# GLA values and GLA gate columns by one 2x2 Strassen product, with the tokens stationary

## The chip, the cores and the metric

The kernel runs on one NeuronCore of a Trainium2 chip. The metric is the device time of one execution in microseconds (us); a few executions are made and their median is given.

## The reference, cut to what matters

One encoder layer on 512 tokens of width 1024. The normalized tokens u meet one wide weight matrix w_in, whose columns feed three branches: gated linear attention (GLA), forgetting attention (FoX), and cross attention into 256 memory tokens. The branches are merged by gates, projected, and a squared-ReLU MLP follows. All of it is float32. For this change, these lines matter:

```python
u = rmsnorm(h, g_mix[l])
proj = u @ w_in[l]
(gq, gk, gv, gg, ga, fq, fk, fv, ff, mq, gates) = split_cols(proj, PROJ_SIZES)
...
o_gla = rmsnorm(o_gla, g_gla_head[l]) * jax.nn.silu(gg.reshape(B, S, GLA_HEADS, GLA_DV))
y_gla = o_gla.reshape(B, S, GLA_V) @ w_gla_o[l]
```

gv (the GLA values) and gg (the GLA output gate) are 512 columns each, for 4 heads of 128. The values enter the attention of each head; its output is normalized per token and head, scaled by a learned gain per channel, and multiplied by silu(gg).

## The kernel before

**Precision by three products.** Every float32 operand of a large product is split into a high part, rounded to the multiplication type float32r, and a low part, the rest. `mm3` (line 163) multiplies high by high, high by low and low by high into one PSUM bank. Of a weight chunk (128 partitions x 1024 numbers, 512 KB), `split_w` (line 150) makes the high part on ScalarE (line 154) and the low part on VectorE (line 155). `load_w` (line 144) loads it through SyncE's (SP's) DMA queue. The pool `weights` has three buffers each for raw, high and low chunks. The tokens u lie in SBUF as high and low halves, `uhi` and `ulo`, transposed: 8 tiles of 128 channels by 512 tokens.

**Two forms of projection.** `gT` (line 168) keeps the weights stationary and streams the 512 tokens: a chunk holds 128 output columns for all 1024 channels, 8 steps of three matmuls. `gN` (line 178) keeps the tokens stationary and streams 512 weight columns: a chunk holds 256 channels of 512 columns, and four chunks make the product for four token tiles. Both are generators that give way after three matmuls; such a step is called a unit.

**The order of the work.** TensorE's instructions run in the order in which the program writes them. `weave` (line 201) does that: it takes a list of steps of an attention branch, and between them draws units from a chain of projections, so many as the steps' shares say. The other engines, the DMA queues of SP and GpSimd (POOL) among them, are put in order by a scheduler at build time, except in stretches marked `in_order`. An instruction may be placed early there, as far as its buffers are free.

The weave of each of the three stages is one call. Lines 754, 865 and 1008:

```python
weave([partial(fn, i) for fn, i, _ in steps], 80, fox_pair(2), gla_k(0), fox_pair(3), gla_q(0), gvg,
...
weave([partial(fn, i) for fn, i, _ in steps], 48, gla_g(0, mp, "th"), gla_g(1, mp, "th"),
      outputs("w_fox_o", ofh, ofl, acc), shares=[n for *_, n in steps])
...
weave([partial(fn, *a) for fn, a, _ in steps], 64, gla_k(1), gla_q(1),
      outputs("w_mem_o", omh, oml, ymem), gla_g(2, lp, "og"), gla_g(3, lp, "og"), shares=[n for *_, n in steps])
```

- FoX (72 to 167 us): 80 units, the last 32 of them the GLA values (`gvg`, line 746, copied out of PSUM by ScalarE).
- Memory attention (167 to 233 us): 48 units, 16 of them the gate columns of two heads.
- GLA (233 to 299 us): 64 units, 16 of them the gate columns of the other two heads.

`gla_g` (line 787) is the gate: a `gT` product of 128 columns, tanh on ScalarE (line 790), and two passes of VectorE (791, 792) that make silu times gain in `sg`, channels on the partitions. In the GLA stage `gla_values` (line 955) makes the heads' outputs with tokens on the partitions and scales each row (line 977) with a reciprocal root from POOL (line 974); `gla_turn` (line 979) transposes them, multiplies by `sg` (line 985) and splits the product for the output projection. `states` (line 921) and `gla_values` read the values `gv`.

**Sums in DRAM.** The branch gates and the MLP are Strassen products already. Their weight sums for the MLP are made in DRAM by transfers in POOL's queue: `sum_ops` (line 107) lists 40, plain copies (line 126) and accumulating ones (line 124) of 0.5 or 1 MB. `next_sum` (line 116) issues them at the pace of the weight splits: none up to the 7th, two with each up to the 16th, one with each from there on. 35 are issued before the branch gates' last round. `u_sum` (line 798) makes the token sums for the branch gates in the memory stage, and `u_lefts` (line 998) and `sum_three` (line 1192) make others from them.

After the GLA stage come the rounds of the branch gates, whose first two weight chunks (`gate_ready`, line 990) are split at the end of the GLA stage.

## Time and profile before

| | |
|---|---|
| three runs | 803.93, 805.38, 807.12 us; median 805.38 |
| the profiled execution | 806.5 us, of which its span from first to last instruction is 804.7 |
| granted TensorE clock | 0.998 of full speed |
| instructions | 11704 |
| chain that ended last | TensorE 89%, VectorE 4%, DMA 3% |
| DMA queues, share of the 16 engines | POOL's (q0) 36.2%, SP's (q1) 33.9%, ScalarE's (q10) 1.4% |

In rows of the profile an engine (PE is TensorE, PEld its weight load, DVE VectorE, ACT ScalarE, POOL GpSimd, SP SyncE) stands with the line of the kernel that recorded the instruction, then output<-input by the program's names, the shape, and a count. Times are us from the start of the span, and us of duration. "idle before" is time in which the engine did nothing before that instruction, and what ended it. A line in a helper, such as 154 or 164, serves many callers.

### The profile page before, as it was taken

What the parts mean: (1) busy time and instruction counts of PE and PEld (TensorE: products, weight loads), DVE (VectorE), ACT (ScalarE), POOL (GpSimd) and SP (SyncE); (2) the same over time, 40 slices, a digit from 0 to 9 for tenths busy, and PEclk for the clock granted to TensorE, in tenths of its full rate; (3) what the DMA queues carried; (4) which work ended last, traced back from release to release, by engine and by line L of the source; (5) the groups of instructions that cost most, each with busy time, mean ns of one, the idle gap of its engine ahead of it and who ended that gap; (6) DMA issues with size and microseconds to landing.
All of it is one profiled execution on the core that took longest, in us unless ns stands there. A gap on an engine that the chain in (4) does not pass through costs nothing.

```text
span 804.7 us, 11704 instructions
## 1 busy us (share of the span) xinstructions
PE 794.1 (99%) x4375; PEld 680.0 (85%) x4375; DVE 601.5 (75%) x951; ACT 459.6 (57%) x733; POOL 91.5 (11%) x129
## 2 busy tenths in 40 slices
PE   9999999999999999999999999999999999999996
PEld 7778888888888878788888889977998899889985
DVE  6877888465654788667764758788799788988896
ACT  7857566443553355556531546864666476647764
POOL 0000102100110122121110000011001100100011
PEclk9999999999999999999999999999999999999999
DMA  9344889994594569797979514998767956795653
GB/s 356 142 157 166 330 299 240 250 287 182 128 235 161 224 194 210 235 219 204 204 163 315 171 58 169 277 237 207 236 182 186 239 206 172 192 283 190 157 89 121
DMA packets 41065, 166.49 MB, mean 207 GB/s; under 512 B 4912, under 2 KB 5616, under 8 KB 38640
## 3 DMA queue, kind: packets, MB, share of 16 engines
q0 software_dynamic: 11072, 62.92, 36.2%
q1 hardware_dynamic: 28576, 98.86, 33.9%
q10 hardware_dynamic: 1360, 3.96, 1.4%
q8 instruction: 34, 0.56, 0.3%
q14 instruction: 23, 0.19, 0.1%
HBM read 163.59 MB, written 35.68 MB: 248 GB/s over the span
## 4 chain that ended last, share of the span: by engine, by line
PE 89%; DVE 4%; DMA 3%; issue 2%; ACT 1%; POOL 1%; POOLq 0%; DVEq 0%; ACTq 0%
PE mm L164 16%; PE mm L165 15%; PE mm L166 15%; PE mm L1330 15%; PE a L165 5%; PE a L166 5%; PE a L164 5%; PE mm L1659 3%; PE mm L385 1%; DMA b<-in_wst_dram 1%; PE mm L1660 1%; PE a L398 1%; PE a L661 1%; DMA raw<-in_wst_dram 1%; PE a L700 1%
## 5 line engine op out<-in xcount | busy, mean ns | idle before, releaser
L155 DVE TENSOR_TENSOR wlo<-raw,whi 128x1024 fp32r<-128x1024 f32 x38 | 46.5, 1223 | 39.4 <-ACT whi L154 39.3
L1389 ACT CAST hi<-raw 128x1024 fp32r<-128x1024 f32 x52 | 54.5, 1048 | 37.5 <-PE mm L1330 17.7
L1390 DVE TENSOR_TENSOR lo<-raw,hi 128x1024 fp32r<-128x1024 f32 x52 | 63.5, 1221 | 14.2 <-ACT hi L1389 13.9
L1330 PE MATMUL mm<-u,hi 128*128 128x256 f32 x384 | 65.1, 283 | 0.0
L154 ACT CAST whi<-raw 128x1024 fp32r<-128x1024 f32 x38 | 39.9, 1050 | 41.2 <-PE mm L165 15.9
L164 PE MATMUL mm<-uhl,whi 128*128 128x512 f32 x144 | 57.7, 400 | 0.0
L1330 PEld LDWEIGHTS mm<-u,hi 128*128 128x128 f32 x384 | 56.8, 191 | 0.3
L166 PE MATMUL mm<-uhl,wlo 128*128 128x512 f32 x144 | 56.3, 391 | 0.0
L165 PE MATMUL mm<-uhl,whi 128*128 128x512 f32 x144 | 56.1, 390 | 0.0
L1709 POOL DMA_DIRECT2D b<-in_wst_dram x30 | 25.7, 856 | 263.4 <-DVE lo L1390 132.9
L165 PE MATMUL mm<-lo,ch 128*128 128x512 f32 (+1 forms) x132 | 51.2, 388 | 0.4 <-DVE lo L1390 0.4
L164 PE MATMUL mm<-hi,ch 128*128 128x512 f32 (+1 forms) x132 | 50.9, 386 | 0.0
L166 PE MATMUL mm<-hi,cl 128*128 128x512 f32 (+1 forms) x132 | 50.9, 386 | 0.0
L1330 PE MATMUL mm<-u2s,hi 128*128 128x256 f32 x288 | 47.6, 283 | 0.0
L1330 PE MATMUL mm<-u,lo 128*128 128x256 f32 x192 | 47.5, 283 | 0.0
L1389 ACT CAST hi<-b 128x1024 fp32r<-128x1024 f32 x26 | 27.2, 1048 | 29.3 <-PE mm L166 18.9
L1330 PEld LDWEIGHTS mm<-u2s,hi 128*128 128x128 f32 x288 | 41.8, 192 | 0.3
L1390 DVE TENSOR_TENSOR lo<-b,hi 128x1024 fp32r<-128x1024 f32 x26 | 31.7, 1221 | 10.7 <-ACT hi L1389 10.7
L165 PE MATMUL a<-lo,ch 128*128 128x512 f32 (+1 forms) x96 | 37.1, 386 | 0.4 <-DVE lo L1447 0.4
L1095 DVE TENSOR_TENSOR lo<-wb,hi 128x1024 fp32r<-128x1024 f32 x21 | 25.3, 1222 | 15.6 <-ACT hi L1091 15.6
L164 PE MATMUL a<-hi,ch 128*128 128x512 f32 (+1 forms) x96 | 37.0, 385 | 0.0
L166 PE MATMUL a<-hi,cl 128*128 128x512 f32 (+1 forms) x96 | 36.9, 385 | 0.0
(506 smaller groups left out, 2296.3 us busy)
## 6 DMA issues: line engine op xcount, KB each, us to landing
raw<-in_wst_dram SPq DMA_DIRECT2D x110, 512.0 KB
raw<-T SPq DMA_DIRECT2D x32, 512.0 KB
b<-in_wst_dram POOLq DMA_DIRECT2D x32, 512.0 KB, 5.4
T<-in_wst_dram POOLq DMA_DIRECT2D x12, 1024.0 KB, 12.6
wb<-in_wst_dram POOLq DMA_DIRECT2D x24, 512.0 KB, 7.8
b<-in_wst_dram SPq DMA_DIRECT2D x16, 512.0 KB
T<-in_wst_dram POOLq DMA_DIRECT2D x12, 512.0 KB, 8.5
wb<-in_wst_dram SPq DMA_DIRECT2D x12, 512.0 KB
```

The lines of the kernel that those rows point to most:

```text
L154: cast = nc.scalar.copy(hi, raw)
L155: low_now[0] = nc.vector.tensor_tensor(lo, raw, f(hi), op=ALU.subtract).ins
L164: nc.tensor.matmul(ps, lh, rh, start=start, stop=False, skip_group_check=on)
L165: nc.tensor.matmul(ps, lh, rl, start=False, stop=False, skip_group_check=on)
L166: nc.tensor.matmul(ps, ll, rh, start=False, stop=stop, skip_group_check=on)
L385: nc.tensor.matmul(kps[h], w[:, h * P:(h + 1) * P], x[:, k, :], start=k == p == 0, stop=k == KT - 1 and p == 2)
L1095: nc.vector.tensor_tensor(lo, source(r, c), f(hi), op=ALU.subtract)
L1330: nc.tensor.matmul(ps[:, a, :], x[:, a, k, :], y[:, s, k, :], start=start, stop=stop, skip_group_check=go is not None)
L1389: split_now[0] = nc.scalar.copy(hi, raw).ins
L1390: split_now[1] = nc.vector.tensor_tensor(lo, raw, f(hi), op=ALU.subtract).ins
L1659: nc.tensor.matmul(ps, wh[:, a, k, :], u[:, k], start=k == 0, stop=False, skip_group_check=True)
L1709: nc.gpsimd.dma_start(to[i], wst[index["B", q, i, x]], accum_op=ALU.add)
```

## The change

The two blocks of 512 columns, gate (gg) and values (gv), are taken as the two column halves of one matrix, the channels as its two row halves, and the tokens as two halves of 256. The 2x2 product is then made from seven products of half size instead of eight (Strassen's scheme in its form with few additions). Each of the seven, `linear(n, left)`, keeps token tiles stationary and streams 512 weight columns: two chunks of weights, two token tiles, 24 matmuls.

- Three products use chunks of w_in as they are (1, 2 and 3), four use weight sums G1 to G4 (2 x 512 KB each) that eight new transfers in POOL's queue make in DRAM. `first_ops` places them among the first of the MLP's sums.
- On the tokens' side, products 1, 2 and 4 use u's halves as they are; 5, 6, 7 and 3 use sums of them, which are added on VectorE and split again. `u_sum`, unchanged in what it computes, is called in the FoX stage now, so its pool opens before FoX. The sums for 7 and 3 are made in the memory stage, in buffers of that stage.
- Products 1, 5, 2, 6 replace the values in FoX's weave (32 units, as before). Products 7 and 3 replace two gate heads in the memory stage's weave (16 units, as before). Product 4 replaces two gate heads in the GLA stage's weave, which goes from 64 to 56 units.
- Evacuation: 1, 2 and 5 are copied by ScalarE; 6, 7, 4 and 3 are added or subtracted by VectorE. Product 2 goes on in product 1's PSUM banks.
- The gate has its tokens on the partitions now. silu is made there by tanh (ScalarE) and one pass of VectorE for each token tile (`gate_half`). It is multiplied in with the row scaling of `gla_values`; the gain, per channel, comes after the transposition in `gla_turn`, where ScalarE makes the high part and one pass of VectorE the low part.
- The gate columns of w_in are stored as four "N" chunks instead of four "T" chunks.

The diff, cut to its core:

```diff
+    def linear_ops():
+        for n, src, add in ((1, "11", 0), (3, "12", 0), (1, "12", 1), (3, "22", 1), (2, 1, 0), (2, "22", 1), (4, 2, 0), (4, "21", 1)):
...
+            yield gsum[n], src, add
...
+    def first_ops():
+        ff, lin = islice(sum_ops(), 35), linear_ops()
+        for own, others in ((2, 0), (1, 1), (1, 1), (1, 2), (1, 2), (1, 2), (1, 26)):
+            yield from islice(lin, own)
+            yield from islice(ff, others)
+        yield from ff
...
+    def factor_tiles():
+        return [gp.tile([P, 4, 256], F32R, tag=tag, name=nm("s")) for tag in ("gv0", "sg2")]
...
+    def linear(n, left):
+        def weights(c):
+            raw = wp.tile([P, 1024], F32, tag="raw", name=nm("raw"))
+            if n in (1, 2, 3):
+                rows, col = {1: (0, "gg"), 2: (4, "gg"), 3: (4, "gv")}[n]
+                src = wst[index["N", "w_in", rows + 2 * c, OFF[col]]]
+            else:
+                src = gsum[{5: 1, 6: 2, 7: 3, 4: 4}[n]][c]
+            nc.sync.dma_start(raw, src)
+            return [x.rearrange("p (k c) -> p k c", k=2) for x in split_w(raw)]
...
+            u, low, high = first_part[t], gv[t], gv[2 + t]
+            if n == 1:
+                nc.scalar.copy(u, ps)
+            if n == 2:
+                nc.scalar.copy(sg[t], ps)
+            if n == 5:
+                nc.scalar.copy(high, ps)
+            if n == 6:
+                vec(u, u, ps)
+            if n == 7:
+                vec(sg[2 + t], u, ps)
+                vec(low, high, u, ALU.subtract)
+                vec(high, high, sg[2 + t], ALU.subtract)
+            if n == 4:
+                vec(sg[2 + t], sg[2 + t], ps)
+            if n == 3:
+                vec(low, low, ps)
...
+        pss = kept[n] = kept[1] if n == 2 else [mmt() for _ in range(2)]
+        for c in range(2):
+            wh, wl = weights(c)
+            for t in range(2):
+                sl = slice(t * P, t * P + P)
+                for kk in range(2):
+                    k = 2 * c + kk
+                    mm3(pss[t], left[0][:, k, sl], left[1][:, k, sl], wh[:, kk, :], wl[:, kk, :], k == 0 and n != 2, k == 3, n in (1, 2))
...
+    def gate_half(t, tt):
+        nc.scalar.activation(tt, sg[t], AF.Tanh, scale=0.5)
+        nc.vector.scalar_tensor_tensor(sg[t], tt, 1.0, sg[t], op0=ALU.add, op1=ALU.mult)
...
-        weave([partial(fn, i) for fn, i, _ in steps], 80, fox_pair(2), gla_k(0), fox_pair(3), gla_q(0), gvg,
+        weave([partial(fn, i) for fn, i, _ in steps], 80, fox_pair(2), once(u_sum, 1), gla_k(0), fox_pair(3), once(early_split, 1),
+              gla_q(0), linear(1, A11r), once(u_sum, 2), linear(5, lambda: early[1]), linear(2, A12r), once(early_split, 2), linear(6, lambda: early[2]),
...
+        temps = {3: other_sum(3)}
+        other(3)
+        def linears():
+            yield from linear(7, s34[3])
+            fo = outputs("w_fox_o", ofh, ofl, acc)
+            temps[4] = other_sum(4)
+            other(4)
+            yield from islice(fo, 16)
+            yield from linear(3, s34[4])
+            gate_halves((0, 1), mp, "th")
+            yield from fo
-        weave([partial(fn, i) for fn, i, _ in steps], 48, gla_g(0, mp, "th"), gla_g(1, mp, "th"),
-              outputs("w_fox_o", ofh, ofl, acc), shares=[n for *_, n in steps])
+        weave([partial(fn, i) for fn, i, _ in steps], 48, linears(), shares=[n for *_, n in steps])
...
-                    nc.vector.tensor_scalar(on[:, t, :], po[e][:, t, :], r[:, t:t + 1], None, op0=ALU.mult)
+                    nc.vector.scalar_tensor_tensor(on[:, t, :], po[e][:, t, :], r[:, t:t + 1], sg[t][:, h * P:(h + 1) * P],
+                                                   op0=ALU.mult, op1=ALU.mult)
...
-            og = lp.tile([P, S], F32, tag="og", name=nm("og"))
-            nc.vector.tensor_tensor(og, pt, sg[h], op=ALU.mult)
-            split(ogh[h], ogl[h], og)
+            nc.scalar.mul(ogh[h], pt, gain_half[:, h:h + 1])
+            nc.vector.scalar_tensor_tensor(ogl[h], pt, gain_half[:, h:h + 1], f(ogh[h]), op0=ALU.mult, op1=ALU.subtract)
...
-        weave([partial(fn, *a) for fn, a, _ in steps], 64, gla_k(1), gla_q(1),
-              outputs("w_mem_o", omh, oml, ymem), gla_g(2, lp, "og"), gla_g(3, lp, "og"), shares=[n for *_, n in steps])
+        weave([partial(fn, *a) for fn, a, _ in steps], 56, gla_k(1), gla_q(1), linear(4, A22r), once(gate_halves, (2, 3), lp, "og"),
+              outputs("w_mem_o", omh, oml, ymem), shares=[n for *_, n in steps])
```

`once` calls a function when the weave reaches it and draws no unit.

More of the change, by code (lines that the diff above doesn't have):

```diff
@@ L45, in chunk_list @@
     L += [("N", "w_in", 2 * j, OFF["gv"]) for j in range(4)]
-    for n, c in (("gg", 4), ("mq", 4)):
-        L += [("T", "w_in", OFF[n] + P * j) for j in range(c)]
+    L += [("N", "w_in", 2 * j, OFF["gg"]) for j in range(4)]
+    L += [("T", "w_in", OFF["mq"] + P * j) for j in range(4)]
     for g, o in (("gate_fox", "w_fox_o"), ("gate_mem", "w_mem_o"), ("gate_gla", "w_gla_o")):
@@ L250, in hybrid_block, with pair_of @@
     gqT = [gp.tile([P, S], F32, name=f"gqT{j}") for j in range(2)]
-    gv = gp.tile([P, NT, 512], F32, name="gv")
-    sg = [gp.tile([P, S], F32, name=f"sg{j}") for j in range(4)]
+    gv, sg = [None] * NT, [None] * NT
+    def pair_of(rows, name, t):
+        x = gp.tile([P, 2, 512], F32, tag=f"{name}{t}", name=nm(name))
+        rows[t:t + 2] = [x[:, i] for i in range(2)]
+    def factor_tiles():
+        return [gp.tile([P, 4, 256], F32R, tag=tag, name=nm("s")) for tag in ("gv0", "sg2")]
+    for t in (0, 2):
+        pair_of(gv, "gv", t)
+        pair_of(sg, "sg", t)
     ofh = [ofp.tile([P, S], F32R, name=f"ofh{j}") for j in range(4)]
@@ L414, in hybrid_block @@
             mem_keys(k)
-        macc, rm = gv[:, 2, :M], gv[:, 1, :2]
-        msq = [gv[:, j, :] for j in range(4)]
+        macc, rm = gv[2][:, :M], gv[1][:, :2]
+        msq = gv[:]
         ms, rx = (small(fp, NT, g) for g in ("ms", "rx"))
@@ L497, in mem_split @@
                                                op1=ALU.subtract)
+    mst = ExitStack()
+    edge = mst.enter_context(pool("edge", side="right"))
+    edge.tile([P, 112], F32, name="edge_pad")
+    xsp = mst.enter_context(pool("sums", side="right"))
+    xsum = {n: xsp.tile([P, 4, 256], F32, name=f"x{n}") for n in (1, 2)}
+    A11r, A12r, A21r, A22r = ([t[:, 4 * k:4 * k + 4, 256 * i:256 * i + 256] for t in (uhi, ulo)] for i in range(2) for k in range(2))
+    A11, A12, A21, A22 = ([f(t) for t in a] for a in (A11r, A12r, A21r, A22r))
@@ new lines, in u_sum, with once @@
+    def u_sum(n):
+        x = xsum[n]
+        if n == 1:
+            nc.vector.tensor_tensor(x, A21[0], A22[0], op=ALU.subtract)
+            nc.vector.tensor_tensor(x, x, A21[1], op=ALU.add)
+            nc.vector.tensor_tensor(x, x, A22[1], op=ALU.subtract)
+        else:
+            nc.vector.tensor_tensor(x, xsum[1], A11[0], op=ALU.subtract)
+            nc.vector.tensor_tensor(x, x, A11[1], op=ALU.subtract)
+    def once(fn, *args):
+        fn(*args)
+        yield from ()
+    kept = {}
@@ L764, in hybrid_block, with om_tile @@
     ogp = mst.enter_context(pool("ogla", side="right"))
-    xsp = mst.enter_context(pool("sums", side="right"))
     omst = ExitStack()
     omp = omst.enter_context(pool("omem", side="right"))
-    omt = [omp.tile([P, 2, S], F32R, tag=f"om{j}", name=f"om{j}") for j in range(4)]
-    omh, oml = ([x[:, i] for x in omt] for i in range(2))
+    omh, oml = {}, {}
+    def om_tile(j):
+        x = omp.tile([P, 2, S], F32R, tag=f"om{j}", name=f"om{j}")
+        omh[j], oml[j] = (x[:, i] for i in range(2))
     def half_of(t, c):
@@ L886, in hybrid_block @@
         stat = small(lp, LINE, "stat")
+        gain_half = stat[:, 64:68]
+        nc.scalar.mul(gain_half, ghead, 0.5)
         def decays(j):
```

74 lines of the change are left out of this document (46 added, 28 removed).

## The prediction

> **What bounds the kernel now.** I read the page first, then TensorE's waits, its pace, and the engines and DMA by stage.
>
> ```profile
> PE 794.1 (99%) x4375; PEld 680.0 (85%) x4375; DVE 601.5 (75%) x951; ACT 459.6 (57%) x733; POOL 91.5 (11%) x129
> ```
>
> Matmul ends are modelled, so 99% alone proves little. The list of what TensorE waited for is complete in four lines:
>
> ```profile
> PE a L296 <- DVE warm L293: 1.2, 1, 1.2
> PE mm L164 <- ACT hi L1091: 0.7, 1, 0.7
> PE a L165 <- DVE lo L1447: 0.4, 1, 0.4
> PE mm L165 <- DVE lo L1390: 0.4, 1, 0.4
> ```
>
> That is 2.7 us in 804.7, none of it in the lines that the change touches. TensorE's own work sets the time, and a removed matmul is worth its pace, not its 390 ns duration. The pace, from two rows of one unbroken stretch:
>
> ```profile
> 238.29 0.39 PE L164 MATMUL mm<-uhl,whi 128*128 128x512 f32 x1
> ...
> 242.82 0.39 PE L166 MATMUL mm<-uhl,wlo 128*128 128x512 f32 x1
> ```
>
> Twenty starts lie between them: (242.82 - 238.29) / 20 = 0.2265 us for a matmul of 512 columns. What the other engines have free, by stage (FoX is from 72 to 167, memory 167 to 233, GLA 233 to 299; the columns after the window and its length are PE, weight loads, DVE, ACT, POOL, clock, DMA share, GB/s):
>
> ```profile
> 40.00:72.00 32.00, 31.89 (x153) 25.44 (x153) 22.64 (x51) 18.91 (x35) 1.56 (x1) 1.00 0.49 166
> 72.00:118.00 46.00, 46.00 (x269) 38.48 (x266) 41.00 (x136) 30.34 (x79) 5.11 (x10) 1.00 0.78 286
> 131.00:167.00 36.00, 36.00 (x191) 30.29 (x190) 18.30 (x47) 18.05 (x37) 5.42 (x7) 1.00 1.03 246
> 167.00:233.00 66.00, 66.00 (x331) 55.95 (x330) 39.48 (x70) 30.66 (x68) 6.07 (x10) 1.00 0.67 201
> 274.00:299.00 25.00, 25.00 (x133) 20.61 (x131) 20.29 (x32) 12.64 (x18) 5.62 (x4) 1.00 0.53 147
> ```
>
> Two things stand out: all 16 DMA engines are full from 131 to 167, and VectorE is busy 20.29 of the last 25 us of GLA.
>
> **The matmuls.** Values and gate columns cost 96 matmuls each now (4 chunks x 24), 192 in all. Seven products of 24 are 168. FoX keeps its 80 woven units (32 of values become products 1, 5, 2, 6) and memory its 48 (two gate columns become 7 and 3). GLA goes from 64 to 56 (two gate columns become product 4). So 24 x 0.2265 = 5.44 us go, all in GLA. The Trainium skill, "TensorE: Matmul & The Clock Gate", section "Wait — 56ns, not 53.3ns?", gives N / 2.4 GHz + 2.5 ns, 215.7 ns at 512 columns: by it the saving would be 5.18. The rows are 5% slower, and the measurement decides. Nothing before the profiled execution's 804.7 us span or behind it changes: 1.8 us lie around it in 806.5, and the median of the runs, 805.38, is 1.1 lower.
>
> **VectorE and ScalarE.** The prices:
>
> ```profile
> L155 DVE TENSOR_TENSOR wlo<-raw,whi 128x1024 fp32r<-128x1024 f32 x38 | 46.5, 1223 | 39.4 <-ACT whi L154 39.3
> L985 DVE TENSOR_TENSOR og<-a,sg 128x512 f32<-128x512 f32 x4 | 2.8, 690 | 1.2 <-PE a L983 0.9
> L791 DVE SCALAR_TENSOR_TENSOR sg<-tt,mm 128x512 f32<-128x512 f32 x4 | 2.7, 681 | 0.7 <-ACT tt L790 0.7
> L1001 DVE TENSOR_TENSOR x<-x,uhl 128x1024 f32<-128x1024 f32 x2 | 2.4, 1218 | 0.0
> L792 DVE TENSOR_SCALAR sg<-sg,cols_s 128x512 f32<-128x512 f32 x4 | 1.9, 480 | 0.0
> L154 ACT CAST whi<-raw 128x1024 fp32r<-128x1024 f32 x38 | 39.9, 1050 | 41.2 <-PE mm L165 15.9 <-issue 12.9 <-PE mm L166 10.0
> L746 ACT COPY gv<-mm 128x512 f32<-128x512 f32 x4 | 2.4, 589 | 2.6 <-PE mm L166 2.6
> ```
>
> FoX gets on VectorE five token-sum passes, moved here from memory (5 x 1.22), two low parts of sums (2.4), four more chunk splits (4.9) and product 6's additions (2 x 0.68): 14.8 us. On ScalarE it gets six casts and two evacuations: 6 x 1.05 + 2 x 0.59 = 7.5. The sums need only the normalized tokens, and 9.4 us of VectorE lie free from 40 to 72 and 17.7 from 131 to 167, so I count nothing. The cover is gone if they fall between 72 and 118, where 5.0 are free: then up to 14.8 - 5.0 = 9.8.
>
> Memory on VectorE: minus the five passes (6.1) and two old gate evacuations (2 x (0.68 + 0.48) = 2.3); plus four passes for the other sums (4.9), two low parts (2.4), two more chunk splits (2.4), eight evacuation passes and two gate halves (10 x 0.68). That is +8.1 in 66 us with 26.5 free: nothing. Weights through ScalarE rise by two casts, again with room.
>
> GLA on VectorE: product 4's two additions and two gate halves (2.7) against two old gate evacuations (2.3) and four multiplications at L985 (2.8): lighter by 2.4. The row scaling at L977 becomes a form with one more operand; no row shows it at 128 columns. I take no difference, since that step is short; 16 instructions at even double their 0.28 would add 4.5, and they are part of the chain below.
>
> **The end of GLA.** Here the cover shrinks.
>
> ```profile
> 279.52 0.94 PE L965 MATMUL a<-mid,qpos 64*128 64x128 f32 x12
> ...
> 287.35 0.80 PE L983 MATMUL a<-cst_s,on 128*128 128x128 f32 x4
> ...
> 292.79 0.60 PE L983 MATMUL a<-cst_s,on 128*128 128x128 f32 x4
> ```
>
> ```profile
> 286.64 1.13 DVE L977 TENSOR_SCALAR on<-a,stat 128x128 f32<-128x128 f32 x4 [0.31 <-POOL stat L974]
> ...
> 289.87 1.13 DVE L977 TENSOR_SCALAR on<-a,stat 128x128 f32<-128x128 f32 x4 [0.30 <-POOL stat L974]
> ```
>
> Ten units stand between head 2's values and its transposes, which begin at 287.35 while L977 still writes their last slices (to 287.77): no slack. With shares of 61, the old order gives 64x55//61 - 64x45//61 = 57 - 47 = 10 units, the new one 50 - 41 = 9; behind it 7 become 6. Each is 3 x 0.2265 = 0.68 less cover. Between 0 (the 2.4 us that VectorE loses lie in this chain) and 1.4 I take 0.6. The second gate_fox chunk now takes the buffer of a w_mem_o chunk that is read until two units before the end; 2 x 0.68, the transposes (0.6) and the six matmuls of the first chunk (1.36) leave 3.3 us for a split of 2.3. It costs nothing, or up to 2.3 if ScalarE's queue is late.
>
> **The weights in FoX.** This is the large unknown. Values take their 96 matmuls from 136.0 to 162.7 (one of three is at L164):
>
> ```profile
> 136.00:162.70 26.70, 12.65 (x32) 5.93 (x32) 1.00 1.04 245
> ```
>
> They need 4 chunks in that time; the four products need 8, one in 3.3 us. How fast SP's queue (q1) can bring 512 KB beside POOL's sums (q0) is in this window, 142.5 to 154.5 (packets, MB, share of the engines):
>
> ```profile
> q0 software_dynamic: 290, 2.00, 80.0%
> q1 hardware_dynamic: 277, 1.04, 22.9%
> ```
>
> 1.04 MB in 12 us is two chunks, 6.0 us each, the two queues taking turns one for one (290 to 277 packets). A load is issued when the low part of three chunks earlier has freed its buffer:
>
> ```profile
> 138.06 1.22 DVE L155 TENSOR_TENSOR wlo<-raw,whi 128x1024 fp32r<-128x1024 f32 x1
> ...
> 139.31 6.44 SPq L147 DMA_DIRECT2D raw<-in_wst_dram  x2
> ```
>
> That split belongs to the third chunk behind the point where values start, so five chunks are issued before 139 in either kernel. The sixth would start at 142.5, where the old one's packets start, and land at 148.5, the next at 154.5, 160.5, 166.5, 172.5; with 1.05 + 1.22 for the split they are ready at 150.8, 156.8, 162.8, 168.8, 174.8. TensorE's order wants them at 152.3, 157.6, 160.3, 164.5 and 169.9 (the last two are memory queries of 5.4 us each). Late by 0, 0, 2.5, 4.3, 4.9: 4.9 us of stall if the sums press all the time. Do they? The change puts eight transfers of 1 MB into POOL's queue ahead of the feed-forward sums:
>
> ```profile
> 80.81 1.24 POOL L126 DMA_DIRECT2D T<-in_wst_dram  x2 [14.56 <-ACT whi L154]
> 84.48 0.97 POOL L126 DMA_DIRECT2D T<-in_wst_dram  x2 [2.43 <-ACT whi L154]
> 93.44 0.97 POOL L126 DMA_DIRECT2D T<-in_wst_dram  x2 [8.00 <-ACT whi L154]
> 103.19 0.97 POOL L126 DMA_DIRECT2D T<-in_wst_dram  x2 [8.78 <-ACT whi L154]
> 111.52 0.97 POOL L126 DMA_DIRECT2D T<-in_wst_dram  x2 [7.37 <-ACT whi L154]
> 121.39 1.65 POOL L124 DMA_DIRECT2D T<-in_wst_dram  x2 [8.90 <-ACT whi L154]
> 127.24 1.65 POOL L124 DMA_DIRECT2D T<-in_wst_dram  x2 [4.20 <-ACT whi L154]
> 138.32 1.63 POOL L124 DMA_DIRECT2D T<-in_wst_dram  x2 [9.43 <-ACT whi L154]
> ...
> 164.78 0.52 POOL L126 DMA_DIRECT2D T<-T  x1 [5.13 <-ACT whi L154]
> ```
>
> L126 is plain copies, L124 adds. Two go with each split up to the 16th, then one. The first row is the eighth split. G1 and G3 take it and a place each at 84 and 93, G2 one at 103 and one at 111, G4 one at 127 and one at 138; so the splits of 121 and 127 carry copies instead of adds, and nothing is piled up at 138. From 138 to 167 the queue holds 3 MB of copies, G4's add and 3 MB of old adds. At 2.0 MB in 9.6 us of engine time an add costs 4.8 per MB; a copy costs 2.95, worked out below; six loads cost 1.4 each: 8.9 + 19.2 + 8.2 = 36 us of work in 29. So it presses, but without a backlog at the start. Between 0 and 4.9 I take 2.4.
>
> **Sum.** -5.4 + 0.6 + 2.4 = -2.4: the profiled execution goes from 806.5 to 804.1, the median from 805.4 to **803.0**.
>
> **Rivals.** *Loads in time* (nothing late in FoX): for it speaks that no load delayed TensorE at 1.03 DMA share before, casts running about three chunks ahead. 805.4 - 5.4 + 0.6 = 800.6.
>
> *Loads late all the way* (4.9 with the one-for-one turns): 805.5, the whole gain returned.
>
> *Copies ahead of weights*, slower. Plain copies go in larger pieces. From 112.5 to 118.4, with a weight load issued at 112.52:
>
> ```profile
> q0 software_dynamic: 48, 2.10, 98.5%
> ...
> q1 hardware_dynamic: 2, 0.01, 0.4%
> ```
>
> Two copies of 1 MB (5.9 us, 2.95 each) let next to nothing of that load through. The rows above show no copy sent from 121 to 164; now the split at about 139 sends two. If they stand whole before the seventh load, the 4.9 become 10.8 and the time 805.4 - 5.4 + 0.6 + 10.8 = 811.4. It decides once more than 9 us are late in all. Against it: the seventh load can slip in behind the first pieces. The Trainium skill speaks on its side: "DMA: Bandwidth & Descriptors", section "Queues, rings and completion order", says that each DMA engine goes round the queues with work packet by packet, and finishes a packet before it changes. The 290 to 277 agree on taking turns; that a big piece holds the engine is the window above.
>
> That the change does not do what it says is excluded by the count: 7 products of 24, no other matmul added.
>
> **How the numbers follow.** The three runs differ by 0.4%, so about 0.5%, 4.0 us, can be told from no change. Chances: loads in time 0.33, forecast 0.35, late all the way 0.17, copies ahead 0.15. Faster than 801.35 are most of the first (0.29) and a fifth of the second (0.07): 0.36. Over 809.4 lie the last and a little of the DVE case: 0.16. The rest is 0.48. The forecast's own range is 801 to 805; 8 in 10 reach from 799.5 (all 5.4 saved, with 0.5 of scatter) to 808.0, which leaves out the last rival and little else.
>
> **What would show it.** 168 matmuls of these columns at 0.2265; TensorE idle behind ACT or DVE splits (L154, L155) between 155 and 185, with the DMA share near 1.0 and casts released by a DMA; about 0.6 us at L983. No such waits means the first rival. A stall before 118 would mean VectorE's sums, and a start of the gate rounds that is not about 2.4 us earlier than 293 would make the forecast wrong.

## The result, and the profile after

The changed kernel takes 840.34 us (median of four runs, 838.52 to 840.75), the kernel before 805.79 beside it: a ratio of 1.0426, 95% interval 1.0400 to 1.0452. Slower by 34.6 us, where 803.0 was forecast. The profiled execution's span is 839.0 us, 34.3 more than before. In the experiments below, e16 and e18 had one execution each at a far lower granted clock (0.655 and 0.556); it is left out of their ratios, and since e16's was the profiled one, e16 has no shifts in the table.

The page after, first its engines, then the slices of TensorE's clock and of the DMA engines, then the chain that ended last:

```profile
PE 799.8 (95%) x4351; PEld 680.7 (81%) x4351; DVE 620.4 (74%) x969; ACT 470.7 (56%) x746; POOL 94.8 (11%) x137
...
PEclk9999978999999999999999999999999999999998
DMA  9345995799966957979888842697857875896643
...
PE 71%; DMA 15%; DVE 7%; ACT 3%; issue 3%; POOL 0%; POOLq 0%; DVEq 0%; ACTq 0%; SPq 0%
```

The 24 matmuls are gone (4375 to 4351). VectorE and ScalarE did 19 and 11 us more, about as worked out, and are no bound: their shares fell by a point. But DMA holds 15% of the chain, where it held 3%, and the list of TensorE's waits, which had nothing over 1.2 us, now begins so:

```profile
PE mm L771 <- DVE PTl L236: 13.5, 1, 13.5
PE mm L182 <- ACT whi L172: 2.9, 1, 2.9
PE a L182 <- DVE pl L236: 2.7, 1, 2.7
PE mm L183 <- DVE wlo L173: 2.4, 4, 0.9
PE a L184 <- DVE ql L236: 1.6, 1, 1.6
```

Where the time went is read by comparing the start of the same step in both traces. For the start and the end of GLA, before and after (the last turn of before, at 292.79, is in the prediction):

```profile
233.31 0.94 PE L891 MATMUL a<-cst_s,la 128*128 128x128 f32 x7
```

```profile
267.54 1.05 PE L1019 MATMUL a<-cst_s,la 128*128 128x128 f32 x8
...
321.99 0.60 PE L1112 MATMUL a<-cst_s,on 128*128 128x128 f32 x4
```

GLA starts 34.2 us later and ends 29.2 later: it is 5.0 us shorter, nearly what was forecast (5.44 saved, 0.6 returned). The loss lies in front of it. Step by step, the shift grows by +2.4 up to FoX's first scores (70 us before), by +16.3 at the scores of pair 2 (112 before), by +5.9 up to the last values of FoX and by +9.6 in the memory stage; then -5.0 in GLA, +2.4 up to the end of the gate rounds, and 2.7 in what follows. The last two, 5.1 us in all, no run takes apart.

**The 16.3 us.** VectorE's timeline and TensorE's at that place, and the link of the chain:

```profile
125.02 0.76 DVE L754 TENSOR_TENSOR nFb<-nFb,cst_s 128x128 f32<-128x128 f32 x2 [12.73 <-DMA nFb<-dF]
125.70 0.68 DVE L818 TENSOR_TENSOR oT<-a,th 64x512 f32<-64x512 f32 x1
126.30 1.27 DVE L236 TENSOR_TENSOR PTl<-a,PTh 128x512 fp32r<-128x512 f32 x2
```

```profile
127.95 0.58 PE L771 MATMUL mm<-Kh,Qh 64*128 64x256 f32 x1 [13.51 <-DVE PTl L236]
```

```profile
100.56 24.43 DMA nFb<-dF
```

The scores of pair 2 need a PSUM bank that the low part PTl of the turn before has yet to read. PTl stands on VectorE behind the mask add on nFb, the broadcast decay rows of pair 2, which ScalarE's queue was asked for at 99.9 and 100.6. VectorE works in order; the mask add waits 12.73 us for the transfer, and all behind it waits too. The granted clock makes 13.5 into 16.3; after the wait it is 0.50, then 0.87 (the column before the last two). TensorE was busy 3.04 us at the first and 9.00 at the second, which loses an estimated 0.50 x 3.04 + 0.13 x 9.00 = 2.7 us:

```profile
127.00:131.00 4.00, 3.04 (x21) 3.05 (x23) 3.60 (x13) 1.23 (x6) 0.00 (x0) 0.50 0.34 91
131.00:140.00 9.00, 9.00 (x39) 7.02 (x37) 6.38 (x25) 5.94 (x16) 0.66 (x2) 0.87 0.48 146
```

The broadcast took 24.4 us. What the queues did meanwhile (packets, MB, share of the engines' time; from 100.5 to 125):

```profile
q0 software_dynamic: 390, 5.55, 75.0%
q1 hardware_dynamic: 302, 1.06, 12.9%
q10 hardware_dynamic: 288, 1.05, 12.8%
```

Before, from 97.5 to 105, with no adds yet in POOL's queue:

```profile
q10 hardware_dynamic: 284, 1.04, 40.0%
q0 software_dynamic: 62, 0.98, 34.8%
```

Nearly the same 1.04 MB went in 7.5 us. After, 288 packets of the broadcast stand beside 390 of q0's and 302 of q1's, and one of q0's is 14 KB on average (5.55 MB / 390) where the broadcast's is 3.6. Where all three queues had work they took turns one for one, as from 112 to 115 us:

```profile
q0 software_dynamic: 32, 1.05, 88.5%
q10 hardware_dynamic: 32, 0.13, 11.4%
q1 hardware_dynamic: 32, 0.13, 10.6%
```

Each queue sent 32 packets in these 3 us, so the broadcast moved 0.13 MB while q0 moved 1.05.

**The 5.9 and 9.6 us.** In ScalarE's list of waits from 60 to 340 us the casts of weights (L172, L154 before), which waited for no DMA before, now do; and the chain shows loads of 512 KB that took 10 to 18 us:

```profile
ACT whi L172 <- DMA raw<-in_wst_dram: 25.0, 9, 5.0
...
ACT whi L172 <- DMA raw<-G: 13.3, 4, 5.5
```

```profile
157.99 10.20 DMA raw<-in_wst_dram
170.63 12.86 DMA raw<-in_wst_dram
185.84 18.05 DMA raw<-in_wst_dram
206.24 11.94 DMA raw<-in_wst_dram
```

Here too the clock adds to the waits: of the 5.9 us TensorE stood for 3.7 (2.92 before a high part at 179.07, 0.76 before a low part at 180.33), and from 179 to 190 the granted clock was 0.84.

**The 2.4 us.** VectorE between 44 and 52 us, and TensorE:

```profile
44.75 1.23 DVE L544 TENSOR_TENSOR x<-x,uhl 128x1024 f32<-128x1024 f32 x1
45.89 1.22 DVE L173 TENSOR_TENSOR wlo<-raw,whi 128x1024 fp32r<-128x1024 f32 x1
...
50.62 1.22 DVE L545 TENSOR_TENSOR x<-x,uhl 128x1024 f32<-128x1024 f32 x1
51.75 0.68 DVE L699 TENSOR_TENSOR Kl<-mm,Kh 128x512 fp32r<-128x512 f32 x1
```

```profile
47.16 0.50 PE L183 MATMUL mm<-wlo,uhl 128*128 128x512 f32 x1 [0.88 <-DVE wlo L173]
...
52.49 0.50 PE L182 MATMUL mm<-whi,uhl 128*128 128x512 f32 x1 [1.17 <-DVE Kl L699]
```

Token-sum passes (L543 to L548), which no matmul reads before 161.6, went at 41 to 57, ahead of the low parts of a weight chunk and of K, and TensorE stood for both.

### The profile page after: what moved, and what is told of

Same layout as the page of the kernel before. It is cut to its first block, busy times and chain, and to the rows that moved or that the text cites. A ratio compares the mean times of both kernels' runs of the same rounds, so it can differ in the third digit from the quotient of the medians.

```text
span 839.0 us, 11711 instructions
## 1 busy us (share of the span) xinstructions
PE 799.8 (95%) x4351; PEld 680.7 (81%) x4351; DVE 620.4 (74%) x969; ACT 470.7 (56%) x746; POOL 94.8 (11%) x137
## 3 DMA queue, kind: packets, MB, share of 16 engines
q0 software_dynamic: 11776, 71.31, 38.6%
## 4 chain that ended last, share of the span: by engine, by line
PE 71%; DMA 15%; DVE 7%; ACT 3%; issue 3%; POOL 0%; POOLq 0%; DVEq 0%; ACTq 0%; SPq 0%
PE mm L1458 13%; PE mm L182 12%; PE mm L183 12%; PE mm L184 12%; DMA raw<-in_wst_dram 10%; PE a L184 4%; PE a L183 4%; PE a L182 4%; DMA nFb<-dF 3%; PE mm L1787 3%; DMA b<-in_wst_dram 1%; PE mm L413 1%; DVE wlo L173 1%; PE mm L1788 1%; PE a L426 1%
## 5 line engine op out<-in xcount | busy, mean ns | idle before, releaser
L173 DVE TENSOR_TENSOR wlo<-raw,whi 128x1024 fp32r<-128x1024 f32 x44 | 53.8, 1222 | 45.8 <-ACT whi L172 45.6
L172 ACT CAST whi<-raw 128x1024 fp32r<-128x1024 f32 x44 | 46.2, 1049 | 66.0 <-DMA raw<-in_wst_dram 27.7
L182 PE MATMUL mm<-uhl,whi 128*128 128x512 f32 x112 | 45.8, 409 | 0.0
L184 PE MATMUL mm<-uhl,wlo 128*128 128x512 f32 x112 | 44.4, 396 | 0.1
L183 PE MATMUL mm<-uhl,whi 128*128 128x512 f32 x112 | 44.3, 395 | 0.0
## 6 DMA issues: line engine op xcount, KB each, us to landing
T<-in_wst_dram POOLq DMA_DIRECT2D x12, 1024.0 KB, 12.6
```

The lines of the kernel that those rows point to most:

```text
L172: cast = nc.scalar.copy(hi, raw)
L173: low_now[0] = nc.vector.tensor_tensor(lo, raw, f(hi), op=ALU.subtract).ins
L182: nc.tensor.matmul(ps, lh, rh, start=start, stop=False, skip_group_check=on)
L183: nc.tensor.matmul(ps, lh, rl, start=False, stop=False, skip_group_check=on)
L184: nc.tensor.matmul(ps, ll, rh, start=False, stop=stop, skip_group_check=on)
```

## The experiments

Eighteen runs. The first theory (A): the eight G transfers fill the DMA engines and delay the broadcast, then the weight loads. Rival (B): VectorE's and ScalarE's added work. The table has each kernel's time, its ratio to the kernel before with the 95% interval, and the shift of five starts on TensorE in its profiled execution against the profile of before: FoX's first scores (70.1), values of head 4 (125.9), start of GLA (233.3), last turn of GLA (292.8), first turn behind the gate rounds (423.1).

| kernel | us | ratio (interval) | 70 | 126 | 233 | 293 | 423 |
|---|---|---|---|---|---|---|---|
| the change | 840.3 | 1.043 (1.040 to 1.045) | +2.4 | +18.7 | +34.2 | +29.2 | +31.6 |
| e1 no G | 827.9 | 1.028 (1.026 to 1.030) | +1.9 | +1.9 | +24.6 | +19.5 | +20.5 |
| e2 before, with G | 837.5 | 1.039 (1.035 to 1.043) | +0.3 | +15.2 | +15.2 | +15.2 | +32.9 |
| e3 one per split | 848.5 | 1.053 (1.049 to 1.057) | +2.2 | +2.1 | +15.1 | +10.1 | +38.9 |
| e4 masks late | 837.7 | 1.040 (1.037 to 1.044) | +1.8 | +13.3 | +29.0 | +23.9 | +28.5 |
| e5 G early | 846.2 | 1.052 (1.049 to 1.055) | +6.6 | +18.7 | +41.0 | +36.0 | +36.9 |
| e6 last quarter late | 848.3 | 1.054 (1.049 to 1.059) | +8.6 | +20.1 | +31.9 | +26.9 | +27.9 |
| e7 no sums | 804.6 | 1.000 (0.999 to 1.001) | +1.9 | +1.9 | +2.8 | -2.2 | -1.1 |
| e8 before, no sums | 805.4 | 1.000 (0.999 to 1.002) | -0.5 | -0.5 | -0.5 | -0.5 | -0.4 |
| e9 no G, half pace | 821.1 | 1.019 (1.017 to 1.021) | -0.4 | +0.2 | +15.4 | +10.4 | +12.6 |
| e10 4 KB pieces | 812.7 | 1.009 (1.007 to 1.011) | -0.4 | +0.3 | +7.4 | +2.4 | +7.3 |
| e11 all together | 823.1 | 1.023 (1.020 to 1.025) | +0.1 | +4.5 | +10.9 | +5.9 | +7.0 |
| e12 copies 4 KB | 823.7 | 1.023 (1.020 to 1.025) | -0.5 | +0.7 | +19.6 | +14.6 | +19.7 |
| e13 before, G, 4 KB | 832.1 | 1.033 (1.032 to 1.035) | -0.2 | +0.4 | +7.2 | +7.2 | +26.8 |
| e14 4 KB, masks late | 805.7 | 1.001 (0.999 to 1.004) | +0.4 | +1.1 | +2.1 | -2.9 | -2.0 |
| e15 before, 4 KB | 806.0 | 1.001 (1.000 to 1.002) | +0.1 | +0.1 | +1.6 | +1.6 | +1.5 |
| e16 e14, 5 copies later | 803.4 | 0.998 (0.997 to 0.999) | | | | | |
| e17 e14, sums not held | 809.0 | 1.005 (1.003 to 1.006) | +1.8 | +1.8 | +2.8 | -2.2 | +2.8 |
| e18 as e16 | 802.9 | 0.997 (0.996 to 0.998) | -0.1 | +0.6 | +1.7 | -3.4 | -2.1 |

### Taking G away, adding it to the kernel before, spreading it, moving the wait

e1, no G:

```diff
-            if n in (1, 2, 3):
...
-                src = gsum[{5: 1, 6: 2, 7: 3, 4: 4}[n]][c]
+            rows, col = {1: (0, "gg"), 2: (4, "gg"), 3: (4, "gv"), 5: (0, "gv"), 6: (4, "gg"), 7: (0, "gg"), 4: (4, "gv")}[n]
+            src = wst[index["N", "w_in", rows + 2 * c, OFF[col]]]
...
-    sums = [first_ops(), islice(sum_ops(), 35, None)]
+    sums = [islice(sum_ops(), 35), islice(sum_ops(), 35, None)]
```

> This is the changed kernel without its eight G transfers: products 5, 6, 7 and 4 read plain chunks of w_in in place of the summed ones, so gate and values come out as other numbers, with the same instructions on every compute engine. Theory A (the eight G transfers, 8.4 MB more in POOL's queue, are what costs time: they delay the broadcast of pair 2's decay rows and then the weight loads): the landmarks of pair 2 and of the memory stage move back by nearly all of +16.3, +5.9, +3.8 and +5.8 us, the +2.4 of the token sums at 45 to 51 us stays, the GLA stage keeps its -5.0, and the time is 802 to 808 us. Theory B (VectorE's and ScalarE's added work, the token sums and splits, holds TensorE): the engines' work is unchanged, so the time stays above 825 us.

827.9 us. The stall before pair 2 is gone (+1.9 at 126), so G makes it. But the shift still grows by 22.7 up to GLA, where A had put it down to G as well. A is half right.

e2, the kernel before with `first_ops` and `linear_ops` as in the change, the "gg" chunks replaced by "fv":

> This is the kernel before with the eight G transfers added in POOL's queue, in the order in which the change puts them, and nobody reading their results. Theory A: the broadcast for pair 2 lands some 20 us late, TensorE waits about 13 to 16 us before the scores of pair 2, later weight loads come late too, and the time is 815 to 835 us. Theory B: transfers that nobody waits for leave the compute order as it was; 805 to 809 us.

837.5 us, with none of the change's compute work:

```profile
PE mm L679 <- DVE PTl L236: 12.0, 1, 12.0
PE mm L182 <- ACT hi L1109: 6.7, 2, 4.9
```

A little over the range. The same wait comes, of 12.0 us, and then 17.7 us are lost in the gate rounds. From 126 to 293 nothing is lost: the memory stage's loss does not come from G alone. There are fewer splits before the gate rounds than in the change, so five transfers were still to come when the rounds began.

e3, `2 if chunk_n[0] <= 16 else 1` replaced by `1`:

> This is the changed kernel with one transfer of POOL's queue per weight split from the eighth split on, where the change issues two for each of splits 8 to 16. The 43 transfers then spread over 43 splits, into the gate rounds. Theory A: fewer bytes stand ahead of the broadcast at 100 us (about 4 transfers in place of 8), so the stall before the scores of pair 2 shrinks from 13.5 us to 0 to 6 us, the weight loads of the late FoX and memory stages take under 8 us in place of 10 to 18, and the time is 808 to 822 us, with some us given back in the GLA stage or gate rounds, where the displaced transfers now run. Theory B: 836 to 842 us.

848.5 us, a miss on the total. The stall before pair 2 is gone, as was said (+2.1 at 126), but from there to GLA 13.0 us are lost still (15.5 in the change), and nine transfers reach into the gate rounds, and they cost 28.8 there (+10.1 to +38.9).

e4, the mask adds behind the pair's second turn:

```diff
-            steps += [(T, 2 * j, 5 * more), (V_, 2 * j, 0)] + [(K, j + 1, 0)] * (j < 3) + [(T, 2 * j + 1, 5 * more)]
+            steps += [(T, 2 * j, 5 * more), (V_, 2 * j, 0), (T, 2 * j + 1, 5 * more)] + [(K, j + 1, 0)] * (j < 3)
```

> This is the changed kernel with the mask adds on the broadcast decay rows placed behind the second turn of the pair in place of between the two, so that on VectorE the low parts of that turn no longer stand behind an instruction that waits for the broadcast. If the in-order wait on VectorE is what turns the late broadcast into a stall, the 16.3 us before the scores of pair 2 shrink to between 3 and 10 us, since the scores and the woven products run ahead of the softmax that needs the rows, and the time is 826 to 834 us. Rival (the late broadcast costs the same wherever it is first read, since the softmax of the pair needs it): 836 to 841 us, and the stall shows at the turns of head 4.

837.7 us, in the rival's range, though the stall did shrink by 4.8 us (18.7 - 2.4 = 16.3 at 126 us, here 13.3 - 1.8 = 11.5). TensorE's wait moved to the values in front of that pair's turns:

```profile
PE a L809 <- ACT Pt L783: 9.2, 1, 9.2
```

It is now the softmax that the broadcast, still 24 us long, holds up. While it is so late, the place of the wait is worth no more than that.

### Earlier G, later sums: two failures

e5 issues the G transfers at the first seven splits, and holds the first token-sum pass behind a FoX turn:

```diff
         if chunk_n[0] <= 7:
-            return
+            ops = islice(lin, 2 if chunk_n[0] == 1 else 1)
...
+            with tc.issue_after(live["turn"]):
+                nc.vector.tensor_tensor(x, A21[0], A22[0], op=ALU.subtract)
```

> This is the changed kernel with the eight G transfers moved ahead of the FF sums, one or two per weight split from the first to the seventh split (46 to 72 us, where the engines' DMA share was about 0.5), and the first pass of the token sums held back behind the second FoX turn (some 92 us). Theory C (the region from 84 to 340 us has no DMA time left: G's transfers stall the broadcast, and the FF sums beside twice as many weight loads stall the memory stage, as the kernel without G showed with 24.6 us left at the end of that stage): both gaps at 45 to 51 us go (2.4 us), the stall before the scores of pair 2 goes, the memory stage still loses about 22 us, and the time is 822 to 832 us. Theory B (what was left without G comes from VectorE's or ScalarE's added work): the same time, but with the memory stage's casts released by those engines, not by a DMA.

846.2 us, a miss. Two new waits, one from each edit:

```profile
PE a L796 <- DVE Pt L789: 6.9, 4, 3.6
PE mm L185 <- DVE V L239: 5.4, 1, 5.4
```

```profile
100.00:110.00 10.00, 10.00 (x61) 8.08 (x60) 10.00 (x25) 5.92 (x17) 0.97 (x2) 1.00 1.06 397
```

At 69 us TensorE waits for V, whose split stands behind that of a late weight load. And the held token sums fall at 102 to 116, where VectorE is busy 10.00 of 10 us, so that the softmax is late: the cover that the prediction said would be gone from 72 to 118 was gone there.

e6 also moves the eight sums of the last FF quarter (every fifth of the list) behind the gate rounds:

> This is the kernel with G early and the token sums held back, and moreover with the eight sums of the last FF quarter (8 MB) taken out of the list that runs from 84 us on and put behind the last FF sums of the gate rounds, from about 450 us on. The region from 84 to 340 us then moves about as many bytes as in the kernel before, with some 3 MB more weight loads. Theory C: the memory stage's loss falls from 22 us to between 2 and 10 us, the gate rounds lose nothing, and the time is 803 to 816 us, if the FF stage takes up the 8 MB. Theory B: no change against the kernel with G early, 822 to 832 us.

848.3 us, a miss too. From 126 to 233 it loses 11.8 us where e5 loses 22.3 (2 to 10 was expected), and the stage that takes up the 8 MB loses them again: +27.9 behind the gate rounds, +40.6 at the end.

### No sums at all: what the compute change is worth

e7 and e8 leave out every G and FF sum; the products read plain blocks.

> This is the changed kernel with no transfers of sums at all, neither G nor FF: products 5, 6, 7 and 4, of the change and of the FF stage, read plain weight blocks in place of summed ones, so the output is other numbers; every instruction of the compute engines stays, and so does every weight load. Theory C: without traffic in POOL's queue the twofold weight loads come in time, every landmark from the memory stage on stands at +2.4 us (the token sums at 45 to 51 us) or less, and behind the GLA stage at -1 to -4 us: 797 to 804 us. Theory B (waits of TensorE on VectorE and ScalarE, or weight loads that come too late by themselves, two for each 5.4 us of matmuls): over 812 us.

> This is the kernel before without its FF sum transfers, the FF stage reading plain blocks in place of the summed ones (other numbers come out): the control for the changed kernel without sums. Theory C: the kernel before loses little to these transfers, 798 to 805 us; the changed kernel without sums is 2 to 5 us faster than this one.

804.6 and 805.4 us. With POOL's queue free of sums, no cast up to the end of GLA waits for a weight load in spite of their doubled rate, and rival B falls: every compute instruction of the change is there. But the change is not worth 2 to 5 us either. Shift against shift it loses 2.4 to the token sums, 0.9 in the memory stage, gains 5.0 in GLA and loses 1.1 up to the end of the gate rounds: 0.6 us gained, in the medians 0.9, which the intervals do not tell from nothing.

### What in POOL's queue: its pace, or its pieces

e9 is e1 with `next_sum` called for only one of a product's two splits, and the token sums held behind the decay sums (61 us):

> This is the changed kernel without the G transfers (products 5, 6, 7 and 4 read plain chunks, so gate and values are other numbers), with one difference in the pace: of the two splits of each product only the first issues an FF sum, so that the FF sums go out against TensorE's work at the rate of the kernel before (a chunk of a product serves 12 matmuls, 2.7 us, where a chunk before served 24, and each split issued one sum). The token sums are also held back behind the decay sums, at about 61 us, where VectorE was idle. Theory D (the FF sums are paced by splits, the change has twice as many splits for the same TensorE time, and so doubles the sums' rate beside the doubled loads): without G at the full pace 22 us were lost in the late FoX and memory stages; here 0 to 6 us, and the time is 801 to 809 us. Theory C2 (the weight loads alone, twice as many, meet the FF sums and come late whatever the sums' pace): over 815 us. The hold takes 2 us off the landmarks from 70 us on, if it does what it says.

821.1 us, over D's range and in that of C2. The hold takes the 2 us off. The pace is a part: the growth from 126 up to GLA falls from 22.7 to 15.2, not to 6. Most is something else.

e10 is the whole change, held token sums, and both kinds of transfers cut to 4 KB:

```diff
-                    d = nc.gpsimd.dma_start(to, src, accum_op=ALU.add, max_dma_last_dim=8192)
+                    d = nc.gpsimd.dma_start(to, src, accum_op=ALU.add, max_dma_last_dim=4096)
...
-                    d = nc.gpsimd.dma_start(to, src)
+                    d = nc.gpsimd.dma_start(to, src, max_dma_last_dim=4096)
```

> This is the changed kernel with all its transfers, but those of POOL's queue for the G and FF sums cut into pieces of 4 KB (64 KB for a plain copy and 8 KB for an adding one before), and the token sums held back to about 61 us. Theory E (the engines serve the queues by pieces, so that a broadcast or a weight load with 4 KB pieces gets one piece for 8 or 64 KB of the sums): the broadcast for pair 2 lands within 12 us in place of 24, raw loads within 8 us in place of 10 to 18, and the time is 810 to 828 us. Theory C (the engines have no time left from 84 to 340 us, in whatever pieces): the loads come sooner but the sums later, and the loss moves to the gate rounds, which wait for their own sums: 832 to 845 us.

812.7 us, against 840.3, with G and all bytes. The stretch from 175 to 215 us in e1 and in e10 (PE, weight loads, DVE, ACT, POOL, clock, DMA share, GB/s):

```profile
175.00:215.00 40.00, 30.34 (x123) 23.69 (x122) 24.03 (x34) 15.82 (x26) 5.00 (x7) 0.79 0.88 261
```

```profile
175.00:215.00 40.00, 39.96 (x199) 33.08 (x198) 30.35 (x50) 21.23 (x44) 5.08 (x7) 1.00 1.06 264
```

The engines are fuller in e10 (1.06 to 0.88; a share over 1 means that packets' times overlap) and move as much a second, yet TensorE works 39.96 us of 40. So theory C, that the engines have no time left, falls for this stretch, and E holds: it is not full engines that cost the time, but how long a load waits for its turn among them. From 60 to 340 us the casts of weights wait 10.3 us for loads, where they waited 38.3 in the change. What waits now is the sums: in this stretch they land 23 to 31 us after their issue (medians; 7.5 to 10 in e1), and nobody is waiting for them. The broadcast for pair 2 is there 10.6 us after it was asked for (98.44 to 109.08), within the 12 that E gave it, and that for pair 3 takes 13.6, where pair 2's took 24.4 in the change. The queues during pair 3's broadcast, from 121 to 127, with pieces of 4 KB beside it:

```profile
q0 software_dynamic: 206, 0.80, 60.7%
q10 hardware_dynamic: 208, 0.78, 34.0%
q1 hardware_dynamic: 60, 0.22, 9.3%
```

The Trainium skill, "DMA: Bandwidth & Descriptors", section "Queues, rings and completion order", has the engines go round the queues packet by packet and finish each. The trace agrees: turns are again one for one between q0 and the broadcast (206 to 208), but a turn of q0's is now 3.9 KB (0.80 MB / 206), and the two move as much (0.80 and 0.78 MB).

e11 adds to e10 the half pace, the first G transfers from the fifth split on, and the last quarter's sums behind the gate rounds:

> This is the change with everything that the runs so far point to: 4 KB pieces, one FF sum for each two splits of a product, the first four G transfers at the fourth to eighth split (60 to 84 us, where the engines' DMA share is under 0.5), the sums of the last FF quarter moved behind the gate rounds, and the token sums held back. If Theories D and E both hold, the stalls before the scores of pair 2 and in the memory stage shrink to 0 to 8 us in all and the time is 800 to 812 us. If the bytes alone decide (8.4 MB of G and 3 MB of loads that the kernel before does not have, against 8 MB moved out), 815 to 835 us.

823.1 us, worse than e10 and in the range that was given for the bytes alone: the early G costs 2.7 by 93 us, and the moved sums some 8 behind the gate rounds, as in e6.

### The last steps

e12, only the copies at 4 KB (token sums held as in e10), and e13, e2 with 4 KB pieces:

> This is the changed kernel with the token sums held back and only the plain copies of POOL's queue cut from 64 KB to 4 KB pieces; the adding transfers keep 8 KB. If the 64 KB pieces are what holds the engines against the broadcast and the weight loads, the time is 811 to 818 us, as with both cut (812.7). If the adds with their 8 KB pieces do it, 828 to 839 us. In between, both do.

> This is the kernel before with the eight unread G transfers, and all G and FF sums in 4 KB pieces. With the pieces as they were it took 837.5 us. Theory E (the pieces decide): 806 to 815 us, with no stall over 2 us before the scores of pair 2. Theory C (bytes decide): 825 to 838 us.

e12 takes 823.7: of the 27.6 us between the change and e10, 16.6 come with the copies' pieces and the hold, 11.0 with the adds'. e13 has no stall before pair 2 (+0.4) and 832.1 us, a miss: the loss in the gate rounds (+7.2 to +26.8) stays. POOL's own queue there:

```profile
305.10 0.57 POOL L144 DMA_DIRECT2D T<-T  x1 [6.10 <-ACT hi L1109]
307.81 0.54 POOL L144 DMA_DIRECT2D T<-T  x1 [2.13 <-ACT f0h L1109]
316.91 0.55 POOL L144 DMA_DIRECT2D T<-T  x1 [8.57 <-ACT hi L1109]
318.18 0.89 POOL L1096 DMA_DIRECT2D wb<-in_wst_dram  x1 [0.71 <-DVE lo L1113]
```

Copies left over stand among the gate rounds' own sums (wb), which POOL issues in order, each behind a cast. Smaller pieces did not help that (19.6 us lost here, 17.7 in e2). The loss goes with the transfers left over: nine cost 28.8 us (e3), five these 17.7 and 19.6, and the change, with none (its last copy is at 309.7, its first wb at 316.1), lost 2.4. No run takes them away alone.

e14 is e10 with e4's order of the masks; e15 is the kernel before with 4 KB pieces:

> This is the changed kernel with 4 KB pieces and the token sums held back (812.7 us), and moreover the mask adds on the decay rows placed behind the second turn of each pair. With 4 KB pieces a broadcast still took 13.6 us, for pair 3, and 6.1 us were lost before that pair's scores. If VectorE's in-order wait makes that stall, it falls to 0 to 2 us and the time is 806 to 810 us; if the softmax needs the rows at the same time anyway, 811 to 814 us.

> This is the kernel before with its FF sums in 4 KB pieces: the control for the changed kernel with 4 KB pieces. The kernel before without any sums took 805.4 us, so there is nothing to win: 803 to 808 us. If smaller pieces cost the engines time by themselves, over 808 us.

805.7 and 806.0 us. VectorE waits for no broadcast any more in e14, and the growth of 6.1 us at pair 3 is gone. In e15 VectorE waits 2.6 us for pair 3's broadcast, where the kernel before waited for none, and its shift of 1.5 comes there: smaller pieces do not shorten every wait. e14's runs go from 803.7 to 810.5; the shifts in the table are those of the fastest.

e16 moves five plain copies (4 MB) of the fourth FF group from the end of the first list to the list behind the gate rounds; e17 is e14 with the token sums free again; e18 is e16 once more:

```diff
-        ff, lin = islice(sum_ops(), 35), linear_ops()
+        ff, lin = islice(sum_ops(), 30), linear_ops()
...
-    sums = [first_ops(), islice(sum_ops(), 35, None)]
+    sums = [first_ops(), islice(sum_ops(), 30, None)]
```

> This is the changed kernel with 4 KB pieces, the token sums held back and the masks placed late (805.7 us, its runs between 803.7 and 810.5), and moreover the five plain copies for the FF sums' fourth group (4 MB) taken from the end of the first list, where they come just ahead of the gate rounds, to the list behind the gate rounds. From 84 to 290 us the engines' DMA share was 0.98, so the runs may scatter by stalls there; with 4 MB less it should fall to about 0.9. If what is left is such pressure: 801.5 to 804 us, faster than the kernel before. If there is nothing more to win: 804 to 807 us. If the copies do harm behind the gate rounds, as 8 MB of the last quarter's sums did: 807 to 813 us.

> This is the same kernel (4 KB pieces, masks placed late; 805.7 us) with the token sums where the change has them, free to run from 41 us on. If they cost TensorE the two gaps at 45 to 51 us, the landmarks from 70 us on move by +1 to +2.4 us and the time is 806.5 to 808.5 us; if something later takes that up, 805 to 806.5 us.

> This is the kernel with 4 KB pieces, late masks, held token sums and the five copies behind the gate rounds once more (803.4 us), for a profile of it. If pressure on the DMA engines ahead of the gate rounds was what the five copies cost, the start of the gate rounds shows no wait for a load, the first turn behind the gate rounds stands at -2.5 to -4 us, and the time is 802 to 804.5 us.

e16 takes 803.4 us and e18 802.9 (805.05 and 804.75 before beside them): the change, in other company, is faster than the kernel before by 0.2 and 0.3%. The kernel before with the same masks and the same five copies moved was not run, so how much of this belongs to the change is not shown. Nor is the reason for the last step: e18's time lies in the expected range, but its two signs failed (in the gate rounds a cast still waits 4.3 us for a load and TensorE 0.7 for that cast, and the first turn behind them stands at -2.1, not -2.5 to -4), and the two profiles, of e14's fastest execution and of e18's 803.9, are of one length (801.9 and 802.1), so that they do not show where the 2.8 us between the medians lie. The stretch from 84 to 290 us in the kernel before, e14 and e18:

```profile
84.00:290.00 206.00, 206.00 (x1152) 173.33 (x1151) 136.92 (x299) 101.02 (x208) 29.40 (x44) 1.00 0.76 231
```

```profile
84.00:290.00 206.00, 205.60 (x1148) 171.83 (x1149) 149.59 (x320) 111.42 (x220) 36.59 (x53) 1.00 0.98 285
```

```profile
84.00:290.00 206.00, 205.62 (x1150) 171.93 (x1150) 149.55 (x318) 111.46 (x221) 33.86 (x48) 1.00 0.92 264
```

G and the added weight loads raise the DMA share of this stretch from 0.76 (0.79 with 4 KB pieces, e15) to 0.98; five copies less bring 0.92. e17 takes 809.0, 3.2 more than e14. The token sums shift the first scores by 1.8, as expected; why it then also loses 5.0 from the last turn of GLA to the end of the gate rounds, where e14 loses 0.9, is not settled (its profiled execution, 810.7, is among its slower ones, e14's the fastest). But e17 is e4 with 4 KB pieces and nothing else, so those two kernels show what the pieces alone are worth: 837.7 to 809.0, 28.7 us, with no stall before pair 2 (+1.8 at 126 in place of +13.3).

## Why the prediction was wrong, point by point

- **The matmuls and the end of GLA**: the matmuls right: 24 gone, GLA 5.0 us shorter for 4.8 forecast; 5.0 or 5.1 in every profiled kernel that has the change's compute work. The 0.6 taken off at the transposes did not come: in the whole stage TensorE stands only once, 0.32 us before the low part of a w_mem_o chunk. That 4.8 came so close is in this part luck.
- **"The weights in FoX"**: here is the step that failed. It weighed the G transfers against SP's weight loads alone, and from 139 us on. By its own words G1 and G3 take places at 81, 84 and 93 us and G2 at 103 and 111, adds among them, and there, at 98 to 105, runs the broadcast of the decay rows on ScalarE's queue; it asked neither what else was in transit nor what VectorE's order puts behind that transfer's first reader. That cost 16.3 us, for 0, and without G (e1) it is gone. It took "nothing is piled up at 138" for the end of the question.
- **"Weights through ScalarE rise by two casts, again with room"** (memory): that is true of ScalarE and says nothing of the loads. The FF sums, now paced by twice as many splits for the same matmuls (half the pace takes 7.5 of 22.7 us off, e9), filled the engines there too (a share of 1.03 from 190 to 220 us), and loads on the chain took 12 and 18 us: +9.6 us, for 0.
- **The loads' delay in late FoX**, forecast +2.4 (0 to 4.9): +5.9. Mechanism right, size over its bound: TensorE stood for 3.7 us, inside it; the lower granted clock behind the wait (0.84 over 11 us, an estimated 0.16 x 11 = 1.8 us) was no term of the sum.
- **VectorE's sums, counted at nothing**: they cost 2.4 us, not between 72 and 118, where the bound looked, but at 45 to 51. "9.4 us of VectorE lie free from 40 to 72" is an average; on the in-order engine a single pass stood ahead of each of two low parts that TensorE wanted at once. Held to 61 us they leave a shift of 0.2 to 1.1 at 126; held to 102 they landed in the stretch that the prediction had named as full.
- **"Copies ahead of weights", the slower rival**: its mechanism, a big piece that holds the engine, is what e10, e12 and e17 showed. It was priced for two copies at one place, 811.4, where it acts on every transfer beside POOL's queue from 84 to 330 us; and the adds' 8 KB pieces do it too (11.0 us).
- **What would show it**: casts released by a DMA came, as said. A stall before 118 came too (from 114.4 on), but by a DMA, not by the sums; the list had no line for that.

What the transfers cost is shown by e7 and e8 (without sums the change takes 35.8 us less, the kernel before no less). That the pieces' size makes the waits is shown by e4 against e17, where nothing else differs, and by e10 and e12, with the sums held; that VectorE's order turns a late broadcast into a stall, by e14 against e10.

## What to carry to other kernels

Before a transfer is added to a queue, list every transfer that will be under way beside it, on every queue, with its first reader and what stands behind that reader on its in-order engine; a mean share of free time answers none of this. Where background transfers share the DMA engines with loads that someone waits for, cut them to the loads' own packet size first: 28.7 us came back that way alone (e4 to e17). With held token sums, the reader moved behind the work that does not need it, and five copies moved clear of the next stage besides, the change went from 4.3% slower to 0.3% faster. And cost background work that is paced by a count (one transfer per split) anew when the change alters the count.

## What the runs showed of the hardware

- DMA engines at a share of 1.06 served TensorE with 0.04 us of idle time in 40 (e10, 175 to 215 us); at 0.88 with larger pieces they let it stand for 9.7 of 40 (e1).
- Smaller pieces cost little: q0 took 38.6% of 839.0 us for 71.31 MB in the change, 40.6% of 812.8 in e10, 324 and 330 us of all engines.
- The queues took turns one for one by packets while they had work, at both packet sizes: 32, 32 and 32 in 3 us of the change, 206 to 208 in 6 us of e10.
- A stall cost more than its length: after 13.5 us of waiting the mean granted clock was 0.50 over 4 us and 0.87 over the next 9, and the shift was 16.3.
